# Pacing transfers from small ScalarE copies in the first gated product of an encoder layer

## The chip, the cores and the metric

One Trainium2 chip, one of its cores. The metric is the device time of one execution of the whole layer in microseconds (us), as a median over runs. TensorE multiplies, VectorE and ScalarE do elementwise work, GpSimd and SyncE issue transfers here. In profile rows they are PE, DVE, ACT, POOL and SP.

## The reference

One layer in float32: 512 tokens, width 1024, hidden width 2816.

```python
def rmsnorm(x, g):
    y = xf * lax.rsqrt(jnp.mean(xf * xf, axis=-1, keepdims=True) + EPS)
    return y * g
def swiglu_ffn(x, w_gate, w_up, w_down):
    return (jax.nn.silu(x @ w_gate) * (x @ w_up)) @ w_down
...
x = x + 0.5 * swiglu_ffn(rmsnorm(x, ffn1_norm[l]), ffn1_w_gate[l], ffn1_w_up[l], ffn1_w_down[l])
x = x + hybrid_mixer(...)     # chunked attention beside trailing-mean pooling
x = x + 0.5 * swiglu_ffn(rmsnorm(x, ffn2_norm[l]), ffn2_w_gate[l], ffn2_w_up[l], ffn2_w_down[l])
x = rmsnorm(x, final_norm[l])
```

The change is in the two up products, `x @ w_gate` and `x @ w_up` with what makes their operands; nearly all that moves is in the first.

## The kernel before, in words

**Precision.** Each float32 matrix is split into a high and a low part. ScalarE casts the high part (L684 in the up product), VectorE subtracts it to get the low part (L147). A product is three matmuls: high by high, high by low of the tokens, low of the weights by high.

**The up product** (`ffn_up`). There are 22 tiles of the hidden width, in the order `down.order`. The first two are begun together while tokens and weights still land. The next, up to `plain` (5 in the first up product, 4 in the second), are plain: two weight panels W(n,0) (gate) and W(n,1) (up), 48 matmuls of 512 columns for each. From tile 5 on, seven block products of 256 columns (a Strassen-like scheme: operands A11, S1, S2 and so on of the tokens, and 11, 13, 24, 22 of the weights) take the place of eight: 84 matmuls a tile. For them VectorE forms an odd sum (L969) and an even one (L972, L973) of each tile's weights. Tiles 5 to 12 are "listed"; the rest follow in an order written out by hand.

**What sets the order.** In the plain and listed tiles a planner (`Work`) takes jobs with an engine, a cost, a rank and their dependencies, gives each ScalarE and VectorE job a latest start (`latest`), makes that its rank, and plays the list through once. The order in which jobs start there is the order of instructions on each engine; at run time each engine takes its queue in order. A load is a job of `sp` with a lag until it lands.

**The normalisation.** The tokens' squares (ScalarE, L743 and L746) are added on VectorE (L749), split (L824, L827), averaged over channels by two matmuls (L517), and turned into the factor `rb` by ScalarE (L524 to L526) and VectorE (L530, L534). VectorE's evacuations and the block operands need `rb`.

**The down weights' sums.** The block scheme of the down product needs sums of blocks of the down weights. They are made in DRAM by transfers which GpSimd issues: a copy and then an accumulating one into the same `wsum`. `make_sums(after)` issues one portion (one to three transfers) behind a "mark": a GpSimd copy (L1298) of one element of `after`, so that the portion starts no earlier than `after` is written. In the first product `after` was `rb`, five block operands, the `t` tile of each plain tile from 2 on (its finished activation), and the `t` tile of each listed tile (its first read of the accumulator). The pool of `t` tiles has eight slots; a slot is free for its next use when all reads of it are done, the mark's too.

Of the kernel before, what the change touches and what calls it, by code (L numbers as in the profile page):

```python
# [8 lines left out]
F32 = mybir.dt.float32  # L9
# [7 lines left out]
P = 128  # L17
# [41 lines left out]
FIRST_BYTE = 1.8  # L59
RAW_LAG = 8.0  # L60
MORE = 6
MIX_ENGINES = {
    mybir.EngineType.PE, mybir.EngineType.DVE, mybir.EngineType.Activation, mybir.EngineType.Pool,
}
# [2 lines left out]
def layer(  # L67
# [31 lines left out]
    nc = tc.nc  # L99
# [138 lines left out]
    class Job:  # L238
        def __init__(self, no, engine, cost, rank, emit, after, gets, uses, lag, chunk):
            self.engine, self.cost, self.rank, self.emit = engine, cost, rank, emit  # L240
            self.after = [z for z in after if z is not None]
            self.gets, self.uses, self.lag, self.chunk = list(gets), list(uses), lag, chunk
            self.no, self.then, self.waits, self.ready = no, [], len(self.after), 0.0
            self.spare, self.seat, self.t0 = 0.0, 0.0, None

    class Work:

# [15 lines left out]
        def latest(self, rooms):  # L263


            t, users, first = 0.0, {}, {}
            row = sorted((z for z in self.jobs if z.engine == "pe" and z.rank >= 10.0), key=lambda z: z.rank)
            for z in row:
                z.by = t
                t += z.cost  # L270
            for z in self.jobs:
                for key in z.uses:
                    users.setdefault(key, []).append(z)
                for what, key in z.gets:
                    if key not in first.setdefault(what, {}):
                        first[what][key] = z
            further = {}
            for what, n in rooms.items():
                got = first[what]
                if what == "bank":  # L280
                    keys = sorted(got, key=lambda key: getattr(got[key], "by", got[key].seat))
                else:
                    keys = list(got)
                for key, later in zip(keys, keys[n:]):
                    for z in users.get(key, ()):
                        further.setdefault(z.no, []).append(got[later])

            def start_by(z):
                if not hasattr(z, "by"):
                    z.by = None  # L290
                    ends = [start_by(k) - (0.0 if k.engine == z.engine else self.hop) for k in z.then + further.get(z.no, [])]
                    end = min([*ends, t + z.spare])
                    z.by = end - z.cost - z.lag
                return z.by

            for z in self.jobs:
                start_by(z)
                if z.engine in ("act", "dve"):
                    z.rank = z.by
            return t  # L300

        def plan(self, room, free):
# [327 lines left out]
    def ffn_up(norm, wA, down, loaded, in_order, plain, turns=(), early=()):  # L630
# [109 lines left out]
        def square(k, before):  # L740
            def first():
                norm.acc = tpool.tile([P, S], F32, tag="acc", name=name("acc"), bufs=1)
                nc.scalar.activation(norm.acc, x[k], AF.Square)  # L743

            def emit():
                nc.scalar.activation(buf["sq", k], x[k], AF.Square)  # L746

            def add():
                nc.vector.tensor_tensor(norm.acc, norm.acc, buf["sq", k], op=ALU.add)  # L749

            if before is None:
                return job("act", 0.56, rank["acc"], first, [at_x[k], gain_in])
            z = job("act", 0.56, rank["acc"] + k, emit, [at_x[k]], [("t", ("sq", k))])
            return job("dve", 0.61, rank["acc"] + k, add, [z, before], uses=[("sq", k)])

        def chunk(kp):
# [90 lines left out]

        placed = {}

        def add_sums(f, done):  # L850
            k, second = down.pair(f)
            if second:
                job("dve", 0.78, rank["second"], lambda: down.sums(f), [done, placed[k]])
            placed[k] = done

        def evacuate(n, f, gate, up, after):
            g, sg = ("g", n), ("sg", n)
            z = job(
                "dve", 0.62, rank["evac"],
                lambda: nc.vector.tensor_tensor(  # L860
                    natural(buf[g]), ordered(buf[gate]), natural(norm.rb), op=ALU.mult
                ),
                [at_rb, *after], [("t", g)], [gate],
            )
            z = job(
                "act", 0.57, rank["evac"], lambda: nc.scalar.activation(buf[sg], buf[g], AF.Silu),
                [z], [("t", sg)], [g],
            )
            z = job(
                "dve", 0.61, rank["evac"],  # L870
                lambda: nc.vector.tensor_tensor(buf[sg], buf[sg], norm.rb, op=ALU.mult), [z],
            )
            done = job(
                "dve", 0.61, rank["place"], lambda: down.place(f, ordered(buf[up]), buf[sg]), [z],
                uses=[up, sg],
            )
            add_sums(f, done)
            if n >= 2:
                job("pool", 3.2, n, lambda: down.make_sums(buf[sg]), [done])

        for i in range(2):
            evacuate(i, down.order[i], ("first", 2 * i), ("first", 2 * i + 1), at_first[2 * i : 2 * i + 2])
# [7 lines left out]
            job("pool", 2.8, 0, lambda k=k: put_aside(buf["turned", k], k), [z], uses=[("turned", k)], lag=3.5)  # L890

        freed = [None] * KD
        for n in range(2, plain):
            f, lows = down.order[n], []
            for j in range(2):
                key = ("W", n, j)
                kind = ("praw", "wraw")[j % 2 == 0]
                z = load(wA[2 * f + j], lambda key=key: buf[key][:, :1024], 0.45, 1.3, [(kind, key)])
                lows.append(
                    split_jobs(key, lambda key=key: buf[key][:, :1024], 1024, rank["plain"], [z], [key])  # L900
                )
            units = [(k, j) for k in range(KD) for j in range(2)]
            if n < plain - 1:
                units.sort(key=lambda u: u[1])
            last = [None] * 2
            for k, j in units:

                def unit(n=n, k=k, j=j):
                    w = buf["part", ("W", n, j)]()
                    mm3(buf["plain", n, j], cut(w, k * P, P), norm.h[k], k == 0, k == KD - 1)  # L910

                last[j] = job(
                    "pe", 0.648, filler(), unit, [lows[j][1], last[j]],
                    [("bank", ("plain", n, j))], [("part", ("W", n, j))],
                )
                if n == plain - 1 and j:
                    freed[k] = last[j]
            evacuate(n, f, ("plain", n, 0), ("plain", n, 1), last)
# [5 lines left out]
        used = {k: [turned[k]] if k in turned else [] for k in range(KD)}  # L924
        at_a = norm.blocks(down.pool, aside, work, at_rb, used, freed)

        if not loaded:
            for i, (z, after) in enumerate(
                (
                    (at_rb, lambda: norm.rb),  # L930
                    (at_a[S3][0][0], lambda: work.buf["whole", S3][0][:, 0].bitcast(F32)),
                    (at_a[A11][0][0], lambda: norm.a[A11][0][0].bitcast(F32)),
                    (at_a[S2][0][0], lambda: work.buf["whole", S2][0][:, 0].bitcast(F32)),
                    (at_a[A22][0][0], lambda: norm.a[A22][0][0].bitcast(F32)),
                    (at_a[S1][0][0], lambda: norm.a[S1][0][0].bitcast(F32)),
                )
            ):
                job("pool", 3.2, 1 + 0.1 * i, lambda after=after: down.make_sums(after()), [z])

        raws, w = {}, {}  # L940

# [84 lines left out]
        def operands(n):  # L1026
# [2 lines left out]
            raw = ("raw", n)  # L1029
            at_raw = job(  # L1030
                "sp", 0.9, n_loads[0] + n, lambda: fetch_into(buf[raw], down.order[n]), [],
                [("praw", raw)], lag=2.6 if n < plain + 2 else RAW_LAG,
            )

            def made(i, src, cols, deps, uses):
# [20 lines left out]
        def half_tile(n):  # L1056
# [34 lines left out]

            p = multiply(acc, 11, 0, A11, True, [])
            u_lo = read(u, 0, acc, 1.0, [p])
            job("pool", 3.2, n, lambda: down.make_sums(buf[u][:, :HT]), [u_lo])
            p = multiply(up_hi, 13, S, S3, True, [])
            z_hi = read(z, 1, up_hi, -1.0, [p])
            p = multiply(acc, 24, 0, S2, False, [u_lo])
# [136 lines left out]
    class Down:  # L1234
# [56 lines left out]
        def make_sums(self, after):  # L1291

            at = self.n_sums
            self.n_sums += 1
            part = self.steps[self.bounds[at] : self.bounds[at + 1]]
            with tc.manual_schedule(engines={mybir.EngineType.Pool}):
                mark = small.tile([P, 16], F32, tag="mark", name=name("mark"))
                nc.gpsimd.tensor_copy(mark[:, 0:1], after[:, 0:1])  # L1298
                for _, at, i, g in part:
                    nc.gpsimd.dma_start(  # L1300
                        self.rows(i, g), self.rows(self.terms[i][at], g),
                        **(dict(accum_op=ALU.add) if at else {}),
                    )
# [1258 lines left out]
```

## Time and profile before

| | us |
|---|---|
| median of 3 runs | 806.54 (806.04 to 808.33) |
| the profiled execution | 802.69 |
| its span, from the first to the last instruction | 800.9 |
| TensorE busy | 790.1 |
| VectorE busy | 712.4 |
| ScalarE busy | 498.7 |
| GpSimd busy | 158.5 |

The first up product runs from the start to about 205 us, its listed part to about 136; the second from about 483. Timeline rows give start, duration, engine, line, operation, output and inputs, and in brackets the engine's idle time just before and what ended it. Waits give the sum, the count and the longest. Rows of stretches give length, busy time (and instructions), granted clock, share of the transfer engines and GB/s.

### The profile page before, as it was taken

What the parts mean: (1) busy time and instruction counts of PE and PEld (TensorE: products, weight loads), DVE (VectorE), ACT (ScalarE), POOL (GpSimd) and SP (SyncE); (2) the same over time, 40 slices, a digit from 0 to 9 for tenths busy, and PEclk for the clock granted to TensorE, in tenths of its full rate; (3) what the DMA queues carried; (4) which work ended last, traced back from release to release, by engine and by line L of the source; (5) the groups of instructions that cost most, each with busy time, mean ns of one, the idle gap of its engine ahead of it and who ended that gap; (6) DMA issues with size and microseconds to landing.
All of it is one profiled execution on the core that took longest, in us unless ns stands there. A gap on an engine that the chain in (4) does not pass through costs nothing.

```text
span 800.9 us, 14970 instructions
## 1 busy us (share of the span) xinstructions
PE 790.1 (99%) x5706; PEld 746.2 (93%) x5706; DVE 712.4 (89%) x1117; ACT 498.7 (62%) x858; POOL 158.5 (20%) x246
## 2 busy tenths in 40 slices
PE   9999999999999999999999999999999999999996
PEld 7889899999999999888888888899999999988986
DVE  7899899999988998777699799999999999986997
ACT  7556565555666665557769555455666555766584
POOL 0035321122220000232254245021110011200010
PEclk9999999999999999999999999999999999999998
DMA  8469977698898765585655867145774467869642
GB/s 298 149 170 308 284 214 196 164 240 198 227 280 288 219 201 162 173 264 117 163 191 107 185 178 212 57 151 194 174 186 165 159 173 176 260 238 339 215 140 106
DMA packets 73992, 158.57 MB, mean 198 GB/s; under 512 B 6576, under 2 KB 31680, under 8 KB 73536
## 3 DMA queue, kind: packets, MB, share of 16 engines
q1 hardware_dynamic: 49952, 109.09, 40.3%
q0 software_dynamic: 23680, 48.24, 28.1%
q8 instruction: 45, 0.74, 0.4%
q10 hardware_dynamic: 288, 0.27, 0.1%
q14 instruction: 27, 0.22, 0.1%
HBM read 153.38 MB, written 50.34 MB: 254 GB/s over the span
## 4 chain that ended last, share of the span: by engine, by line
PE 85%; DVE 2%; DMA 1%; issue 1%; ACT 0%; SPq 0%; ACTq 0%; DVEq 0%
PE mm L217 12%; PE mm L219 12%; PE mm L218 12%; PE mm L226 10%; PE a L218 9%; PE a L217 9%; PE a L219 9%; PE a L226 6%; DMA raw<-wsum 1%; PE mm L2005 1%; PE mm L2095 1%; PE a L2069 1%; DVE parts L147 1%; PE mm L2069 0%; PE a L2095 0%
## 5 line engine op out<-in xcount | busy, mean ns | idle before, releaser
L147 DVE TENSOR_TENSOR parts<-raw,parts 128x1024 fp32r<-128x1024 f32 (+2 forms) x129 | 137.3, 1078 | 14.3 <-ACT parts L141 12.2
L1018 ACT ACTIVATE t<-mm 128x256 f32<-128x256 f32 x93 | 35.8, 385 | 86.6 <-PE mm L219 59.7
L141 ACT CAST parts<-raw 128x1024 fp32r<-128x1024 f32 (+1 forms) x60 | 59.3, 993 | 32.7 <-DMA raw<-wsum 10.3
L1298 POOL COPY mark<-t 128x1 f32<-128x1 f32 x40 | 24.9, 622 | 268.1 <-DVE t L1193 149.5
L1300 POOL DMA_DIRECT2D wsum<-in_wB_dram x72 | 73.0, 1146 | 12.6 <-DMA wsum<-wsum 7.5
L684 ACT CAST parts<-raw 128x1024 fp32r<-128x1024 f32 (+2 forms) x69 | 59.8, 883 | 17.8 <-PE a L218 8.0
L147 DVE TENSOR_TENSOR wlo<-raw,whi 128x1024 fp32r<-128x1024 f32 (+1 forms) x41 | 46.8, 1141 | 6.3 <-ACT whi L141 4.3
L147 DVE TENSOR_TENSOR ah<-acts,ah 128x512 fp32r<-128x512 f32 (+1 forms) x72 | 47.1, 663 | 3.0 <-ACT ah L141 2.9
L141 ACT CAST ah<-acts 128x512 fp32r<-128x512 f32 (+1 forms) x72 | 41.0, 583 | 8.6 <-PE mm L218 6.1
L219 PE MATMUL mm<-ha,parts 128*128 128x256 f32 x152 | 41.9, 276 | 0.8 <-DVE parts L147 0.8
L1598 DVE TENSOR_TENSOR parts<-raw,parts 128x1024 fp32r<-128x1024 f32 x24 | 29.6, 1239 | 14.7 <-ACT parts L1593 14.7
L217 PE MATMUL mm<-ha,parts 128*128 128x256 f32 x152 | 41.8, 275 | 0.0
L218 PE MATMUL mm<-ha,parts 128*128 128x256 f32 x152 | 41.8, 275 | 0.0
L1593 ACT CAST parts<-raw 128x1024 fp32r<-128x1024 f32 x24 | 25.2, 1048 | 25.9 <-PE a L218 7.1
L226 PE MATMUL mm<-ha,parts 128*128 128x256 f32 x312 | 38.6, 275 | 0.0
L217 PE MATMUL mm<-ah,parts 128*128 128x256 f32 x136 | 37.4, 275 | 0.0
L218 PE MATMUL mm<-ah,parts 128*128 128x256 f32 x136 | 37.4, 275 | 0.0
L219 PE MATMUL mm<-ah,parts 128*128 128x256 f32 x136 | 37.4, 275 | 0.0
L226 PEld LDWEIGHTS mm<-ha,parts 128*128 128x128 f32 x312 | 36.8, 192 | 0.1
L1018 ACT ACTIVATE t<-a 128x256 f32<-128x256 f32 x47 | 18.1, 384 | 29.5 <-PE a L226 21.2
L963 DVE TENSOR_TENSOR parts<-wsum,parts 128x1024 fp32r<-128x1024 f32 x26 | 31.7, 1219 | 2.6 <-ACT parts L958 2.6
L226 PE MATMUL a<-ha,parts 128*128 128x256 f32 x264 | 32.6, 275 | 0.0
(410 smaller groups left out, 3013.6 us busy)
## 6 DMA issues: line engine op xcount, KB each, us to landing
raw<-in_wA_dram SPq DMA_DIRECT2D x86, 512.0 KB, 5.1
wsum<-in_wB_dram POOLq DMA_DIRECT2D x60, 512.0 KB, 7.7
raw<-wsum SPq DMA_DIRECT2D x36, 512.0 KB, 4.9
raw<-in_wB_dram SPq DMA_DIRECT2D x30, 512.0 KB, 4.9
wsum<-wsum POOLq DMA_DIRECT2D x20, 512.0 KB, 4.8
x<-in_xT_dram SPq DMA_DIRECT2D x16, 256.0 KB, 5.3
raw<-in_wQK_dram SPq DMA_DIRECT2D x8, 512.0 KB, 4.1
wsum<-in_wB_dram POOLq DMA_DIRECT2D x12, 256.0 KB, 7.6
```

What stands on the lines that cost most here:

```text
L141: nc.scalar.copy(hi, src)
L147: nc.vector.tensor_tensor(lo, src, hi.bitcast(F32), op=ALU.subtract)
L217: nc.tensor.matmul(acc, a[0], high, start=start, stop=False, **more)
L218: nc.tensor.matmul(acc, a[0], low, start=False, stop=False, **more)
L219: nc.tensor.matmul(acc, a[1], high, start=False, stop=stop, **more)
L226: nc.tensor.matmul(acc, a[1 if i == 2 else 0], moved, start=start, stop=stop, **more)
L684: "act", c_high, rank_of, lambda: nc.scalar.copy(pair()[0], src()),
L963: nc.vector.tensor_tensor(lo, src, hi.bitcast(F32), op=ALU.subtract)
L1018: nc.scalar.activation(natural(dst), ordered(src), AF.Copy, scale=scale)
L1300: nc.gpsimd.dma_start(self.rows(i, g), self.rows(self.terms[i][at], g), **(dict(accum_op=ALU.add) if at else {}),)
L1593: return lambda: nc.scalar.copy(buf["part", i][0], buf["raw", i])
L1598: nc.vector.tensor_tensor(lo, buf["raw", i], hi.bitcast(F32), op=ALU.subtract)
```

## The change

`pace` adds a 128x1 copy on ScalarE, from what a portion of sums follows, to a tile of its own with four slots; the mark reads that tile. In the first product the portions now follow the high parts of the plain weights from W(2,1) on (five), four block operands (S3, S2, A22, S1), and the listed tiles' first reads (eight): 17 as before. In the second they follow W(2,0), W(3,0) and the eight listed tiles. The small copies are taken from the list as soon as their input is written (`at_once`). The squares, their sums and the mean get a rank 10 us earlier. The first two squares wait for a weight cast. The lag of the first two listed loads in the list goes from 2.6 to 8.0 us. The mark's tile is 8 elements wide and not 16.

```diff
+EARLY_MEAN = 10.0
...
-                    z.rank = z.by
+                    z.rank = -1e3 if z.at_once else z.by - EARLY_MEAN * (z.rank < -5.0 and z.rank >= -19.0)
...
-                return job("act", 0.56, rank["acc"], first, [at_x[k], gain_in])
-            z = job("act", 0.56, rank["acc"] + k, emit, [at_x[k]], [("t", ("sq", k))])
+                return job("act", 0.56, rank["acc"], first, [at_x[k], at_w[0][0][0]])
+            then = at_w[0][3][0] if k == 1 else None
+            z = job("act", 0.56, rank["acc"] + k, emit, [at_x[k], then], [("t", ("sq", k))])
...
+        def pace(at, order, src):
+            n = next(paces)
+            def note():
+                buf["pace", n] = small.tile([P, 1], F32, tag="pace", name=name("pace"), bufs=4)
+                nc.scalar.copy(buf["pace", n], src())
+            z = job("act", 0.22, rank["copy"], note, [at])
+            z.at_once = True
+            job("pool", 3.2, order, lambda: down.make_sums(buf["pace", n]), [z])
...
-            if n >= 2:
-                job("pool", 3.2, n, lambda: down.make_sums(buf[sg]), [done])
...
-        if not loaded:
-            for i, (z, after) in enumerate(
...
-                job("pool", 3.2, 1 + 0.1 * i, lambda after=after: down.make_sums(after()), [z])
+        at_weights = [z for pair in plain_lows[(0 if loaded else 1) :: (2 if loaded else 1)] for z in pair[:1]]
+        if loaded:
+            for i, (z, what) in enumerate(zip(at_weights, plain_keys[::2])):
+                pace(z, i, lambda what=what: buf["part", what](0, 0)[0][:, 0:1].bitcast(F32))
+        else:
+            for i, (z, what) in enumerate(zip(at_weights, plain_keys[1:])):
+                pace(z, i, lambda what=what: buf["part", what](0, 0)[0][:, 0:1].bitcast(F32))
+            for i, what in enumerate((S3, S2, A22, S1)):
+                pace(at_a[what][0][0], 10 + i, lambda what=what: norm.a[what][0][0][:, 0:1].bitcast(F32))
...
-                [("praw", raw)], lag=2.6 if n < plain + 2 else RAW_LAG,
+                [("praw", raw)], lag=RAW_LAG,
...
-            job("pool", 3.2, n, lambda: down.make_sums(buf[u][:, :HT]), [u_lo])
+            pace(u_lo, 20 + n, lambda: buf[u][:, 0:1])
...
-                mark = small.tile([P, 16], F32, tag="mark", name=name("mark"))
+                mark = small.tile([P, 8], F32, tag="mark", name=name("mark"))
```

ScalarE, before, in listed tile 7 (L1018 reads an accumulator into a `t` tile, L1109 and L1116 are the two Silu halves, L684 the casts of the next weights):

```order
L1018 ACTIVATE t_975<-mm_951 128x256 [waits PE_49,Activation_49]
L1109 ACTIVATE t_992<-t_732 128x256 [waits DVE_49,Pool_49]
L1018 ACTIVATE t_997<-mm_967 128x256 [waits PE_49,Activation_49]
L1116 ACTIVATE t_992<-mm_682 128x256
L1018 ACTIVATE t_975<-mm_951 128x256 [waits PE_49]
L1109 ACTIVATE t_1032<-t_860 128x256 [waits DVE_49,Pool_49]
L684 CAST parts<-raw_874 128x512 [waits DMAHW6_49]
```

The same place after:

```order
L1032 ACTIVATE t_998<-a_980 128x256 [waits PE_49]
L858 COPY pace_1004<-t_998 128x1 [waits Activation_49,Pool_49]
L1123 ACTIVATE t_1009<-t_775 128x256 [waits DVE_49]
L1130 ACTIVATE t_1009<-mm_723 128x256
L1032 ACTIVATE t_1026<-mm_995 128x256 [waits PE_49]
L1032 ACTIVATE t_998<-a_980 128x256 [waits PE_49]
L1123 ACTIVATE t_1052<-t_899 128x256 [waits DVE_49]
```

The wait for GpSimd went from the Silus (L1109, now L1123) to the small copy.

VectorE, before, from the last token tile's low part to the low part of the squares' sum (`raw_244`, `raw_276`, `raw_301` are W(2,0), W(2,1), W(3,0)):

```order
L149 SCALAR_TENSOR_TENSOR hlo_315<-x_82,gain_sb,hhi_314 128x512
L147 TENSOR_TENSOR parts<-raw_244,parts 128x1024
L147 TENSOR_TENSOR parts<-raw_276,parts 128x1024
L749 TENSOR_TENSOR acc_182<-acc_182,t_327 128x512
L749 TENSOR_TENSOR acc_182<-acc_182,t_341 128x512
L749 TENSOR_TENSOR acc_182<-acc_182,t_348 128x512
L147 TENSOR_TENSOR parts<-raw_301,parts 128x1024
L827 TENSOR_TENSOR t_372<-acc_182,t_371 128x512
```

The same place after:

```order
L150 SCALAR_TENSOR_TENSOR hlo_311<-x_82,gain_sb,hhi_310 128x512
L750 TENSOR_TENSOR acc_190<-acc_190,t_316 128x512
L750 TENSOR_TENSOR acc_190<-acc_190,t_321 128x512
L750 TENSOR_TENSOR acc_190<-acc_190,t_327 128x512
L750 TENSOR_TENSOR acc_190<-acc_190,t_341 128x512
L148 TENSOR_TENSOR parts<-raw_238,parts 128x1024
L148 TENSOR_TENSOR parts<-raw_271,parts 128x1024
L829 TENSOR_TENSOR t_358<-acc_190,t_357 128x512
L148 TENSOR_TENSOR parts<-raw_303,parts 128x1024
```

The additions went ahead of the low parts of W(2,0) and W(2,1), and the low part of W(3,0) behind the mean's.

VectorE, before, at the end of the listed tiles (L1316, L1317 and L1371 are differences of finished activations; the row `parts<-raw_1515` is the low part of 11 of tile 13):

```order
L972 TENSOR_TENSOR raw_1687<-raw_1664,raw_1515 128x512
L973 TENSOR_TENSOR raw_1687<-raw_1687,raw_1515 128x512
L1105 TENSOR_TENSOR t_1645<-t_1645 128x256
L1316 TENSOR_TENSOR acts_168<-acts_168 128x256
L1317 TENSOR_TENSOR acts_168<-acts_168 128x256
L1086 TENSOR_TENSOR t_1601<-mm_1597,t_1601 128x256
L1086 TENSOR_TENSOR t_1601<-mm_1692,t_1601 128x256
L147 TENSOR_TENSOR parts<-raw_1515,parts 128x512
```

The same place after (`raw_1550` is that tile's):

```order
L986 TENSOR_TENSOR raw_1716<-raw_1703,raw_1550 128x512
L987 TENSOR_TENSOR raw_1716<-raw_1716,raw_1550 128x512
L1330 TENSOR_TENSOR acts_168<-acts_168 128x256
L1331 TENSOR_TENSOR acts_168<-acts_168 128x256
L1385 TENSOR_TENSOR acts_168<-acts_168 128x512
L1119 TENSOR_TENSOR t_1680<-t_1680 128x256
L1100 TENSOR_TENSOR t_1635<-mm_1631,t_1635 128x256
L1100 TENSOR_TENSOR t_1635<-mm_1726,t_1635 128x256
L148 TENSOR_TENSOR parts<-raw_1550,parts 128x512
```

A second L1371 (now L1385) moved from behind that low part to ahead of it; before, it stood seven rows behind.

More of the change, by code (lines that the diff above doesn't have):

```diff
@@ L243, in __init__ @@
             self.no, self.then, self.waits, self.ready = no, [], len(self.after), 0.0
-            self.spare, self.seat, self.t0 = 0.0, 0.0, None
+            self.spare, self.seat, self.t0, self.at_once = 0.0, 0.0, None, False
     class Work:
@@ L848, in ffn_up @@
         placed = {}
+        def pace(at, order, src):
[6 more added lines that the diff above has]
+            job("pool", 3.2, order, lambda: down.make_sums(buf["pace", n]), [z])
+        paces = iter(range(100))
         def add_sums(f, done):
@@ L892, in ffn_up @@
         freed = [None] * KD
+        plain_lows, plain_keys = [], []
         for n in range(2, plain):
-            f, lows = down.order[n], []
+            f, lows = down.order[n], plain_lows[len(plain_lows) :]
             for j in range(2):
@@ L901, in ffn_up @@
                 )
+                plain_lows.append(lows[-1])
+                plain_keys.append(key)
             units = [(k, j) for k in range(KD) for j in range(2)]
@@ L925, in ffn_up @@
         at_a = norm.blocks(down.pool, aside, work, at_rb, used, freed)
-        if not loaded:
-            for i, (z, after) in enumerate(
[L929 to L937, printed above, removed]
-                job("pool", 3.2, 1 + 0.1 * i, lambda after=after: down.make_sums(after()), [z])
+        at_weights = [z for pair in plain_lows[(0 if loaded else 1) :: (2 if loaded else 1)] for z in pair[:1]]
[7 more added lines that the diff above has]
+                pace(at_a[what][0][0], 10 + i, lambda what=what: norm.a[what][0][0][:, 0:1].bitcast(F32))
         raws, w = {}, {}
```

## The prediction

> **What bounds the kernel now.** I read the page's first part, then the waits of TensorE, then busy time by stretches, then the timeline where TensorE stops.
>
> ```profile
> PE 790.1 (99%) x5706; PEld 746.2 (93%) x5706; DVE 712.4 (89%) x1117; ACT 498.7 (62%) x858; POOL 158.5 (20%) x246
> ```
>
> ```profile
> PE mm L226 <- ACT t L1018: 1.9, 1, 1.9
> ...
> PE mm L219 <- DVE parts L147: 0.8, 1, 0.8
> PE mm L226 <- ACT parts L684: 0.3, 1, 0.3
> ```
>
> ```profile
> 80.00:85.00 5.00, 4.86 (x44) 1.00 1.21 230
> 85.00:90.00 5.00, 3.25 (x29) 1.00 1.08 394
> ...
> 135.00:140.00 5.00, 4.15 (x38) 1.00 0.04 13
> ...
> 540.00:550.00 10.00, 10.00 (x92) 1.00 0.69 246
> ```
>
> TensorE is the bound: 790.1 of 800.9 us. In each row of the last fence the fourth number is its busy time in the stretch. It is less than the stretch in three places that matter: two in the first up product (around 85 and 135 us) and 0.3 us at the start. The second up product (540 is inside it) is full, so nothing can be gained there. A change to the first product can win at most these three places.
>
> Around 85 us, engine by engine (start, duration, what, and in brackets the idle time before it and who ended it):
>
> ```profile
> 83.36 1.50 PE L226 MATMUL mm<-ha,parts 128*128 128x256 f32 x12
> 86.75 1.49 PE L226 MATMUL mm<-sa,parts 128*128 128x256 f32 x11 [1.89 <-ACT t L1018]
> ...
> 84.49 0.51 POOL L1300 DMA_DIRECT2D wsum<-wsum  x1 [4.96 <-DMA wsum<-in_wB_dram]
> 84.98 0.20 POOL L1298 COPY mark<-t 128x1 f32<-128x1 f32 x1
> ...
> 80.88 0.38 ACT L1018 ACTIVATE t<-mm 128x256 f32<-128x256 f32 x1 [0.62 <-PE mm L226]
> 85.22 0.42 ACT L1109 ACTIVATE t<-t 128x256 f32<-128x256 f32 x1 [3.96 <-POOL mark L1298]
> 86.32 0.37 ACT L1018 ACTIVATE t<-mm 128x256 f32<-128x256 f32 x1
> ...
> 82.19 1.23 DVE L969 TENSOR_TENSOR raw<-raw 128x1024 f32<-128x1024 f32 x1 [0.25 <-DMA raw<-in_wA_dram]
> 86.17 0.69 DVE L147 TENSOR_TENSOR parts<-raw,parts 128x512 fp32r<-128x512 f32 x1 [1.31 <-ACT parts L684]
> 87.66 1.23 DVE L147 TENSOR_TENSOR wlo<-raw,whi 128x1024 fp32r<-128x1024 f32 x1 [0.80 <-ACT whi L684]
> ```
>
> Read it from the bottom of the chain. GpSimd stands 4.96 us for a sum's transfer; the mark behind it in its queue still has to read a `t` tile (the finished activation of plain tile 4), so that slot is not free; ScalarE's next Silu, L1109, wants the slot and waits 3.96 us; the read of the accumulator behind it in ScalarE's queue, at 86.32, comes late; TensorE waits for it. Twelve products of this shape take 1.34 us (1.50 less the overlap of the last), so TensorE was due at 84.70 and began at 86.75: 2.05 us. VectorE loses 1.31 + 0.80 = 2.11 us to the same block, and 0.25 to a landing.
>
> Around 135 us:
>
> ```profile
> 135.20 0.28 PE L218 MATMUL mm<-ha,parts 128*128 128x256 f32 x1
> 136.32 0.38 PE L219 MATMUL mm<-ha,parts 128*128 128x256 f32 x1 [0.85 <-DVE parts L147]
> ...
> 135.59 0.68 DVE L147 TENSOR_TENSOR parts<-raw,parts 128x512 fp32r<-128x512 f32 x1
> ```
>
> Products start every 0.11 us, so the third was due at 135.31 and came 1.01 us late: VectorE finished its low weights at 136.27, after a queue without a gap since 88.8. VectorE is the second bound of this stage.
>
> **The change part by part.** *Marks read a tile of their own.* No `t` tile is held by GpSimd any more. L1109 then follows its input at about 81.3, the read of the accumulator follows its product (done at 83.4) and is over before 84.70. TensorE regains 2.05 us and VectorE 2.11. The transfers still wait as long; only GpSimd's own queue stands behind them.
>
> *The small copies.* 27 copies on ScalarE (17 in the first product, 10 in the second) take the places of reads that GpSimd did. The nearest row for one is the 128x1 ACTIVATE, the nearest for waiting on one's own engine's last write is a cast:
>
> ```profile
> 30.08 0.20 ACT L441 ACTIVATE table<-t 128x1 f32<-128x1 f32 x1
> ...
> 67.41 1.06 ACT L684 CAST parts<-raw 128x1024 fp32r<-128x1024 f32 x1 [0.35 <-ACT parts L684]
> ```
>
> So 0.20 to 0.55 us each, 3.4 to 9.4 us in the first product. ScalarE is 62% busy, and a copy stands behind the read that feeds TensorE, not ahead of it; the next read is due a product (1.34 us) later. Cost to TensorE: nothing; were that cover gone, up to 0.55 us at each of eight listed tiles. Each copy from the fifth on also waits until GpSimd has read the tile four marks earlier; see the rivals.
>
> *The mean earlier.* Rank minus 10 puts the sums of squares, and the low part of their sum, ahead of the low part of W(3,0) on VectorE; the two mean products stand four products (0.86 us) earlier on TensorE.
>
> ```profile
> 25.09 0.59 PE L517 MATMUL a<-t,mean_of 128*128 128x512 f32 x2
> ...
> 23.11 1.22 DVE L147 TENSOR_TENSOR parts<-raw,parts 128x1024 fp32r<-128x1024 f32 x1
> 24.24 0.69 DVE L827 TENSOR_TENSOR t<-acc,t 128x512 fp32r<-128x512 f32 x1
> 27.86 0.69 DVE L530 SCALAR_TENSOR_TENSOR t<-a,t 128x512 f32<-128x512 f32 x1 [2.93 <-ACT t L526]
> ```
>
> The low part ended at 24.93; with 1.13 us (23.11 to 24.24) less ahead of it, it ends at 23.8, before TensorE's new place at 24.23. So the chain through ScalarE and VectorE's L530 comes about 0.8 us sooner, and VectorE's whole queue behind it, which then runs without a gap. Bounds: 0 (a square comes late) to 0.86.
>
> *The start.* ScalarE casts the quarter weights before the squares; on VectorE the second quarter's low part now stands behind both operations on the second token tile. The page allows a gain of 0.3 (its wait on ACT parts) and a loss of one quarter's 0.42; I take a loss of 0.1 on TensorE. It is hidden: at 135 us TensorE waits for VectorE anyway.
>
> *Later landings (lag 8.0 for the first two listed loads).* They move VectorE's rows, no transfer. The odd sum of listed tile 6 (L969, 1.13 us) passes ahead of the low part of 24 of tile 5:
>
> ```profile
> 60.58 1.50 PE L226 MATMUL mm<-xa,parts 128*128 128x256 f32 x12
> ...
> 58.91 2.35 DVE L147 TENSOR_TENSOR parts<-raw,parts 128x1024 fp32r<-128x1024 f32 x2
> ```
>
> The low part ended near 60.1 and is needed at 60.80 (third product). Now 60.1 + 1.13 - 0.8 = 60.4: 0.4 us to spare. And one `acts` difference (L1371) moves ahead of the low part of tile 13:
>
> ```profile
> 141.93 0.68 DVE L1371 TENSOR_TENSOR acts<-acts 128x512 f32<-128x512 f32 x1
> ```
>
> It costs 0.6 in the queue, between nothing (were VectorE ahead there) and 0.68.
>
> *The second product.* Same edits, full before; 0, from 0 to a loss of 0.5 (a small copy in the wrong place).
>
> *The sum.* It is set by VectorE at tile 13. Its low part ended at 136.27; less 2.11, less 0.8, plus 0.6 gives 133.96, less up to 0.25 if the load of 82.19 lands sooner. TensorE, due at 135.31 - 2.05 + 0.1 = 133.36, then starts about 133.9 instead of 136.32: 2.4 us sooner, of which 0.5 us of waiting is left. Ends: 3.0 (all but the start's 0.1 of 2.05 + 1.01) and 1.9 (0.5 of new short waits on VectorE). After 136 us TensorE is full to the tail, so this carries to the end. The profiled execution took 802.69 us, 3.85 below the median of 806.54; I take the difference off the median: 806.5 - 2.4 = **804.1 us**, and 803.5 to 804.6 for this case.
>
> **Rivals.** *VectorE's new order holds the gain back.* If a late square keeps the mean where it was, the low part of 24 ends at 61.2 and TensorE waits 0.4 at 60.80, and tile 13's comes at 134.76: gain 1.5, **805.0**. For it: the 0.4 us to spare. Against: nothing but one square stands between.
>
> *The sums crowd the first listed loads.* Sums now start near 21 us instead of 29, beside loads that had the queues nearly alone. Loads and sums, transfers started in 20 to 60 us and then in 60 to 90 us, KB each and median to landing:
>
> ```profile
> raw<-in_wA_dram SPq DMA_DIRECT2D x6, 512.0 KB, 4.6
> wsum<-in_wB_dram POOLq DMA_DIRECT2D x6, 512.0 KB, 7.9
> ```
>
> ```profile
> wsum<-in_wB_dram POOLq DMA_DIRECT2D x9, 512.0 KB, 10.3
> raw<-in_wA_dram SPq DMA_DIRECT2D x6, 512.0 KB, 7.3
> ...
> wsum<-in_wB_dram POOLq DMA_DIRECT2D x1, 256.0 KB, 13.4
> ```
>
> ```profile
> 30.44 0.33 SPq L950 DMA_DIRECT2D raw<-in_wA_dram  x1
> 70.92 0.33 SPq L950 DMA_DIRECT2D raw<-in_wA_dram  x1
> ...
> 42.94 1.22 DVE L969 TENSOR_TENSOR raw<-raw 128x1024 f32<-128x1024 f32 x1
> ```
>
> A load in the crowd took 7.3, the worst from 70.92 to its user at 82.19, 11.3 us. The first listed load, issued near 30.9, would at 11.3 land at 42.2, just when VectorE wants it (42.94 - 0.8). At 13.4, the slowest sum, it lands at 44.3: VectorE 2.1 late, and it hardly catches up; **806.2**. Against: few sums are in flight by 31 us. The Trainium skill, "DMA: Bandwidth & Descriptors", section "Issuing engines are not separate DMA queues", says that transfers from all engines run on the same 16 and interleave, which speaks against putting sums here. By an equal share, an estimate from that page and the 4.6 us above, a load beside two sums takes 13.8 us and the time is 806.6. The 7.3 us of the crowded stretch agrees with the direction, not with so large a factor.
>
> *Slower: the block comes back on ScalarE.* With four tiles, a copy waits if GpSimd is over four marks behind, and then not one slot but ScalarE's whole queue stands, once a tile. Each costs what it did at 85 us, 2.05; three make 806.5 + 2 x 2.05 = **810.6**, and three is where it decides. GpSimd falls behind if marks take over a listed tile's 9.38 us (84 products of 0.1117).
>
> ```profile
> 63.84 0.41 POOL L1298 COPY mark<-ha 128x1 f32<-128x1 f32 x1
> 85.73 0.32 POOL L1298 COPY mark<-t 128x1 f32<-128x1 f32 x1
> ```
>
> Between these, with GpSimd behind all the time, five more marks ran: 21.9 us for six steps, 3.65 each. So it catches up; only much slower transfers would do it.
>
> *More than forecast.* The runs' median is 3.85 us above the profiled execution. If part of that is the same block lasting longer when a transfer is slower, the change wins it too: about **801.7**. Nothing in the one profile shows it.
>
> **How the numbers follow.** As forecast 0.50, VectorE's order 0.17, crowd 0.08, slower 0.11, more 0.14. About 0.3% (2.4 us) is what a measurement of this kernel tells from no change, and the forecast lies on that line: a little over half of its 0.50 counts as faster. Faster 0.28 + 0.14 = 0.42; same 0.22 + 0.17 + 0.08 = 0.47; slower 0.11. The range reaches to the crowd above, with the runs' own scatter (806.04 to 808.33), and to the last rival below: 801.0 to 807.2, which leaves out the slower case and the tails.
>
> **What would show it.** Right: no ScalarE wait on a mark, TensorE full from 80 to 90 us, L530 near 27, a wait under 0.8 us for VectorE near 133 to 134, first mark near 21. Wrong: ScalarE copies that wait on GpSimd; VectorE waiting for a landing near 42; TensorE idle near 60; any gap past 480 us.

## The result

The changed kernel takes 801.08 us (median of 6 runs, 800.63 to 801.20), the kernel before, run beside it, 806.04 (median of 5 runs, 803.99 to 808.33): 5.0 us less, a ratio of 0.9937 (95% interval 0.9919 to 0.9954). Three runs in the slow state are left out of the ratios: a sixth one of the kernel before (888.49 us) here, and two of old_sums (814.87 and 815.51) below. The forecast was 804.1 us, with 801.0 to 807.2 as the range. The profiled execution took 800.86 us, against 802.69 before: only 1.83 us less. This difference between 5.0 and 1.83 is what the experiments had to settle.

The profile after. First part, waits of TensorE, and busy time of TensorE by stretches (length, busy time, granted clock, transfers):

```profile
PE 790.6 (99%) x5706; PEld 746.3 (93%) x5706; DVE 712.7 (89%) x1117; ACT 503.9 (63%) x885; POOL 163.1 (20%) x246
...
PE mm L220 <- DVE parts L148: 0.4, 1, 0.4
PE a L219 <- DVE wlo L148: 0.2, 1, 0.2
...
80.00:85.00 5.00, 5.00 (x48) 1.00 0.83 228
85.00:90.00 5.00, 5.00 (x47) 1.00 1.20 192
120.00:130.00 10.00, 9.86 (x89) 1.00 1.13 237
130.00:135.00 5.00, 4.59 (x42) 1.00 0.58 201
...
540.00:550.00 10.00, 10.00 (x92) 1.00 0.58 216
```

The hole at 85 us is closed, and no wait on a mark is left. At 120 to 135 us the busy time is 0.55 us short of the stretches. By the starts of the products, as the prediction counted, the loss there is nearer 1 us: the last record before a stop runs for 0.28 us, though products otherwise start every 0.11 us, so part of each stop counts as busy. Timelines of the places that the forecast spoke of (start, duration, what):

```profile
23.79 0.69 DVE L829 TENSOR_TENSOR t<-acc,t 128x512 fp32r<-128x512 f32 x1
27.19 0.69 DVE L531 SCALAR_TENSOR_TENSOR t<-a,t 128x512 f32<-128x512 f32 x1 [1.57 <-PE mm L227]
42.34 1.22 DVE L983 TENSOR_TENSOR raw<-raw 128x1024 f32<-128x1024 f32 x1
...
120.26 0.68 DVE L1385 TENSOR_TENSOR acts<-acts 128x512 f32<-128x512 f32 x1
131.99 0.68 DVE L1385 TENSOR_TENSOR acts<-acts 128x512 f32<-128x512 f32 x1
133.59 0.68 DVE L148 TENSOR_TENSOR parts<-raw,parts 128x512 fp32r<-128x512 f32 x1
...
24.06 0.96 PE L518 MATMUL a<-t,mean_of 128*128 128x512 f32 x2
122.41 1.91 PE L227 MATMUL mm<-ha,parts 128*128 128x256 f32 x12
133.64 0.28 PE L219 MATMUL mm<-ha,parts 128*128 128x256 f32 x1
134.33 0.38 PE L220 MATMUL mm<-ha,parts 128*128 128x256 f32 x1 [0.41 <-DVE parts L148]
...
21.28 0.37 POOL L1312 COPY mark<-pace 128x1 f32<-128x1 f32 x1 [19.47 <-ACT pace L858]
79.54 0.18 POOL L1312 COPY mark<-pace 128x1 f32<-128x1 f32 x1 [5.12 <-ACT t L1123]
```

L531 came at 27.19 (27.86 before), tile 13's third product at 134.33 (136.32 before), 1.99 us sooner. Three stops are left in these rows: 0.36 us inside the two products of the mean (0.96 us for the pair, 0.59 before), 0.4 us inside the twelve of tile 12 at 122.41 (1.91 us, where such a group takes 1.50), and 0.58 us at tile 13 (due at 133.64 + 0.11 = 133.75). From 79.5 us on GpSimd waits for its marks, so it is no longer behind. The loads of tile weights started in 20 to 60 us now have company (KB each, median to landing):

```profile
wsum<-in_wB_dram POOLq DMA_DIRECT2D x9, 512.0 KB, 8.4
raw<-in_wA_dram SPq DMA_DIRECT2D x6, 512.0 KB, 7.2
```

They landed in 7.2 us instead of 4.6, and VectorE's first user of one, at 42.34, had no idle time before it.

### The profile page after: what moved, and what is told of

Its sections match the earlier page's. It is cut to its first block, busy times and chain, and to the rows that moved or that the text cites. A ratio compares the mean times of both kernels' runs of the same rounds, so it can differ in the third digit from the quotient of the medians.

```text
span 799.1 us, 14937 instructions
## 1 busy us (share of the span) xinstructions
PE 790.6 (99%) x5706; PEld 746.3 (93%) x5706; DVE 712.7 (89%) x1117; ACT 503.9 (63%) x885; POOL 163.1 (20%) x246
## 4 chain that ended last, share of the span: by engine, by line
PE 90%; DVE 6%; issue 1%; DMA 1%; ACT 1%; SPq 0%; DVEq 0%; ACTq 0%
PE mm L218 13%; PE mm L220 13%; PE mm L219 13%; PE mm L227 11%; PE a L218 10%; PE a L219 10%; PE a L220 10%; PE a L227 6%; DVE parts L148 1%; DVE wlo L148 1%; PE mm L2109 1%; PE mm L2019 1%; DMA x<-in_xT_dram 1%; PE a L2083 1%; DVE raw L983 1%
## 5 line engine op out<-in xcount | busy, mean ns | idle before, releaser
L1312 POOL COPY mark<-pace 128x1 f32<-128x1 f32 x27 | 24.7, 915 | 150.3 <-ACT pace L858 145.2
L227 PE MATMUL mm<-ha,parts 128*128 128x256 f32 x336 | 42.2, 275 | 0.1
L220 PE MATMUL mm<-ha,parts 128*128 128x256 f32 x152 | 41.9, 276 | 0.4 <-DVE parts L148 0.4
L218 PE MATMUL mm<-ha,parts 128*128 128x256 f32 x152 | 41.8, 275 | 0.0
L219 PE MATMUL mm<-ha,parts 128*128 128x256 f32 x152 | 41.8, 275 | 0.0
L227 PEld LDWEIGHTS mm<-ha,parts 128*128 128x128 f32 x336 | 39.9, 192 | 0.4 <-DVE parts L148 0.3
L1312 POOL COPY mark<-t 128x1 f32<-128x1 f32 x19 | 6.9, 362 | 157.9 <-DVE t L1207 148.4
```

The lines of the kernel that those rows point to most:

```text
L218: nc.tensor.matmul(acc, a[0], high, start=start, stop=False, **more)
L219: nc.tensor.matmul(acc, a[0], low, start=False, stop=False, **more)
L220: nc.tensor.matmul(acc, a[1], high, start=False, stop=stop, **more)
L227: nc.tensor.matmul(acc, a[1 if i == 2 else 0], moved, start=start, stop=stop, **more)
```

## The experiments

Each was timed against the kernel before on the same chip. Those from one call share the runs of the kernel before, which scattered from 802.27 to 810.49 us in the three calls.

| kernel | us, median (range) | ratio to before (95%) |
|---|---|---|
| before_again | 806.19 (801.95 to 807.12) | 0.9992 (0.9971 to 1.0014) |
| marks_only | 801.42 (799.99 to 803.74) | 0.9945 (0.9927 to 0.9964) |
| direct_marks | 801.06 (800.51 to 801.81) | 0.9941 (0.9918 to 0.9964) |
| mean_later | 800.97 (800.27 to 801.41) | 0.9934 (0.9909 to 0.9960) |
| early_only | 801.36 (800.74 to 802.25) | 0.9950 (0.9932 to 0.9968) |
| old_sums | 813.67 (802.68 to 815.51) | 1.0069 (1.0037 to 1.0102) |
| old_start | 801.01 (800.16 to 801.98) | 0.9938 (0.9913 to 0.9963) |
| sums_later | 800.67 (800.33 to 801.12) | 0.9938 (0.9914 to 0.9962) |
| after_again | 800.96 (800.28 to 801.63) | 0.9941 (0.9922 to 0.9961) |
| last_later | 800.06 (799.71 to 800.89) | 0.9930 (0.9909 to 0.9950) |
| one_tile | 802.41 (801.52 to 803.12) | 0.9953 (0.9935 to 0.9972) |
| marks_one_tile | 810.06 (808.80 to 810.93) | 1.0053 (1.0033 to 1.0073) |

### The kernel before, once more

No edit.

> The kernel before, unchanged, to see another of its executions. The profiled one of 802.69 us lost 2.05 us of TensorE to one block (a Silu of ScalarE that waits for a mark of GpSimd), while the median is 806.3. Theory A (such blocks make the difference too): ratio 1.00, runs scattered over some 4 us, and if the profiled execution is above 804 us, its TensorE waits for ScalarE's L1018 (behind L1109 waiting for a mark) come to more than 1.9 us, up to 1.9 + 3.6. Theory B (the difference has another place): the waits behind marks stay near 1.9 us, and a slower execution loses its time elsewhere, in the down products or at the tail.

Its profiled execution took 807.12 us (span 805.3). Its waits, then ScalarE, TensorE and GpSimd around the block, then TensorE by stretches of 2 us:

```profile
ACT t L1109 <- POOL mark L1298: 5.6, 1, 5.6
ACT t L866 <- POOL mark L1298: 3.0, 1, 3.0
ACT t L1018 <- POOL mark L1298: 1.3, 1, 1.3
...
87.78 0.42 ACT L1109 ACTIVATE t<-t 128x256 f32<-128x256 f32 x1 [5.56 <-POOL mark L1298]
...
73.66 1.50 PE L226 MATMUL a<-ha,parts 128*128 128x256 f32 x12
75.99 1.60 PE L226 MATMUL a<-sa,parts 128*128 128x256 f32 x12 [0.83 <-ACT t L1018]
84.31 1.50 PE L226 MATMUL mm<-ha,parts 128*128 128x256 f32 x12
89.31 2.62 PE L226 MATMUL mm<-sa,parts 128*128 128x256 f32 x12 [3.49 <-ACT t L1018]
91.73 2.15 PE L226 MATMUL mm<-ha,parts 128*128 128x256 f32 x12
93.72 0.39 PE L226 MATMUL a<-xa,whi 128*128 128x256 f32 x2
...
87.05 0.51 POOL L1300 DMA_DIRECT2D wsum<-wsum  x1 [6.46 <-DMA wsum<-in_wB_dram]
87.55 0.20 POOL L1298 COPY mark<-t 128x1 f32<-128x1 f32 x1
...
88.00:90.00 2.00, 0.69 (x4) 0.92 1.17 306
90.00:92.00 2.00, 2.00 (x12) 0.50 1.28 420
92.00:94.00 2.00, 2.00 (x15) 0.73 0.84 299
94.00:96.00 2.00, 2.00 (x20) 1.00 1.20 218
```

It is the block of the prediction in a longer edition. GpSimd waited 6.46 us for a sum's transfer (4.96 in the execution first shown), L1109 5.56 us for the mark, and TensorE, due at 84.31 + 1.34 = 85.65, began at 89.31: 3.66 us. Then comes a price that I had not counted. The granted clock fell to 0.50, and the next two groups of twelve took 2.42 and 1.99 us instead of 1.34 each, 1.73 us more. With 0.99 us at 75.99 (due at 75.00) the blocks cost 6.38 us in this execution, against 2.05 in the first. The Trainium skill, "TensorE: Matmul & The Clock Gate", "What's actually happening", says that an idle window of about 3.4 us halves the clock until TensorE has been busy as long. The trace agrees: the stop of 3.66 us brought 0.50, which was over by 94 us, and the stop of 2.05 us left 1.00. Without the blocks the two executions come out alike: 807.12 - 6.38 = 800.74 us and 802.69 - 2.05 = 800.64. None of its twelve runs was longer than this one, so the median loses less than 6.38. The mean granted clock of the unprofiled runs points the same way: in the 30 runs of the kernel before in this call it was 0.998 to 0.999 in those under 804 us and 0.994 to 0.996 in those from 809 us on. Theory A holds; theory B has nothing for it here.

### Small copies alone

The order of before on all engines, plus 27 copies at the old places (the mark's tile is 8 elements wide here too):

```diff
-                job("pool", 3.2, n, lambda: down.make_sums(buf[sg]), [done])
+                pace(done, n, lambda: buf[sg][:, 0:1])
...
-                job("pool", 3.2, 1 + 0.1 * i, lambda after=after: down.make_sums(after()), [z])
+                pace(z, 1 + 0.1 * i, lambda after=after: after()[:, 0:1])
...
-            job("pool", 3.2, n, lambda: down.make_sums(buf[u][:, :HT]), [u_lo])
+            pace(u_lo, n, lambda: buf[u][:, 0:1])
```

> The kernel before with its order kept on every engine, to which only the 27 small copies are added, at the places where the marks stood, and the marks read them. No earlier sums, no earlier mean, no changed landings. Theory A (the slots that marks held): 801 to 802 us, at most 0.8 above the changed kernel, runs within 1 us of each other, no ScalarE wait on a mark; TensorE waits 0.7 to 0.9 us at tile 13, since VectorE's order is as it was. Theory B (the order and the earlier sums bring it): 805 to 806.5 us, scattered as before.

801.42 us, as theory A said, but the runs scattered over 3.75 us, not within 1. No wait on a mark was left. What TensorE still waits for in the listed tiles is VectorE, and VectorE waits for landings (waits, then one of the two places):

```profile
PE mm L219 <- DVE parts L147: 0.9, 1, 0.9
PE a L226 <- DVE parts L147: 0.7, 1, 0.7
PE a L218 <- DVE wlo L147: 0.6, 1, 0.6
...
82.97 1.23 DVE L983 TENSOR_TENSOR raw<-raw 128x1024 f32<-128x1024 f32 x1 [0.92 <-DMA raw<-in_wA_dram]
```

So the copies alone take the block away. The sums still start late, and loads started in 60 to 90 us took a median of 7.2 us to land (7.3 before). That this crowd makes the scatter is likely, but not shown.

### Earlier sums alone, and marks that read the tiles

Two kernels for the other half. direct_marks is the changed kernel with its order and copies, but the marks read the tiles themselves:

```diff
-            job("pool", 3.2, order, lambda: down.make_sums(buf["pace", n]), [z])
+            job("pool", 3.2, order, lambda: down.make_sums(src()), [z])
```

> The changed kernel with its order kept on every engine, the small copies too, but GpSimd's marks read the cast weights, block operands and t tiles themselves, not the copies. Theory A: holders are blocked again; 803 to 806 us, runs scattered by 2 us or more, and ScalarE or VectorE waits for marks in the profile that stand ahead of TensorE waits. Theory B: the changed kernel's 801.1 us, within 0.5, and runs within 1 us.

801.06 us: my theory A missed here. Marks that hold cast weights, block operands and the first reads of listed tiles cost nothing in this kernel. So a held slot as such is not enough, and theory C followed: GpSimd must also be behind. early_only puts it to the test in the order of before, without a copy:

```diff
-                    (at_rb, lambda: norm.rb),
-                    (at_a[S3][0][0], lambda: work.buf["whole", S3][0][:, 0].bitcast(F32)),
...
+            for i, (z, what) in enumerate(zip([pair[0] for pair in plain_lows[1:]], plain_keys[1:])):
+                job("pool", 3.2, i, lambda what=what: down.make_sums(buf["part", what](0, 0)[0][:, 0:1].bitcast(F32)), [z])
...
-            if n >= 2:
+            if n >= 2 and loaded:
                 job("pool", 3.2, n, lambda: down.make_sums(buf[sg]), [done])
```

> The kernel before with its order kept on TensorE, VectorE, ScalarE and SyncE; only the marks of the first product move to the changed kernel's earlier places (cast weights, block operands), read there directly, without small copies. In the listed tiles they read the t tiles as before. Theory C (two conditions make the block: GpSimd is behind when the listed tiles begin, and a mark holds a slot; taking away either ends it): 801 to 802 us, runs within 1.5 us, no wait of ScalarE on a mark longer than 0.5 us. Rival D (the earlier sums need the changed order or the copies beside them): 803 to 806 us, scattered, with waits on marks.

801.36 us, no wait of ScalarE on a mark. GpSimd in early_only, mark for the first read of tile 7:

```profile
78.73 0.21 POOL L1294 COPY mark<-t 128x1 f32<-128x1 f32 x1 [8.54 <-ACT t L1014]
```

It waited for its tile; in the execution of before shown above, GpSimd was so far behind that the mark of plain tile 4, older than this one, ended at 87.75. Theory C fits: with nothing but copies, or nothing but earlier sums, nearly the whole gain is there, and both together bring little more. One thing is left open. The slot of the block was that of a plain tile's finished activation, and neither direct_marks nor early_only has a mark that reads such a tile. So early_only takes away both the lateness and this hold; earlier sums with the marks of the plain tiles left in place were not tried.

### All but the sums

The changed kernel with marks at the old places, reading the tiles:

```diff
-            pace(u_lo, 20 + n, lambda: buf[u][:, 0:1])
+            job("pool", 3.2, n, lambda: down.make_sums(buf[u][:, :HT]), [u_lo])
```

and likewise at the other places.

> The changed kernel with the marks as before: at the old places, reading the tiles themselves, no small copies. The earlier mean, the start, the landings and the planner stay as changed, so this is all of the change but its handling of the sums. Theory C: 804.5 to 806.5 us, scattered over 2 us or more, with waits on marks as in the kernel before. Rival E (the other edits bring a part of their own): 801.5 to 803.5 us.

813.67 us, slower than before, worse than either theory. ScalarE and TensorE in it, then TensorE by stretches:

```profile
81.58 0.42 ACT L1128 ACTIVATE t<-t 128x256 f32<-128x256 f32 x1 [12.44 <-POOL mark L1317]
82.59 2.93 PE L227 MATMUL a<-ha,parts 128*128 128x256 f32 x12 [11.33 <-ACT t L1037]
...
78.00:80.00 2.00, 0.00 (x0) 0.50 1.22 208
88.00:90.00 2.00, 2.00 (x20) 1.00 1.06 141
```

In the order that came out, the Silu that wants a held slot stands earlier, behind tile 6's first read, and waits 12.44 us. The planner does not know that GpSimd is behind. The loss is not the same in every execution: one of the twelve runs took 802.68 us, two 807 to 808, the others 812 and more. So the other edits bring nothing without the sums, and a block of the same kind took another size. The order on TensorE, VectorE and ScalarE differs from that of the changed kernel as well as from that of before, so the loss against before is that of this order with late sums, not of one edit.

### The earlier mean and the start

mean_later and old_start undo one edit each:

```diff
-EARLY_MEAN = 10.0
+EARLY_MEAN = 0.0
```

> The changed kernel with the earlier rank of the squares and of the mean set to nothing. As I worked it out, VectorE's chain of the mean (L531) comes 0.7 us later, its queue has no gap behind it, and tile 13's low part is later by as much: 801.8 us (801.5 to 802.2), TensorE waiting 1.1 us instead of 0.4 there. Rival (VectorE's queue has slack in between): 801.1 us, no change. Second rival (the low part of 24 of tile 5 comes late too): above 802.2.

```diff
-                return job("act", 0.56, rank["acc"], first, [at_x[k], at_w[0][0][0]])
-            then = at_w[0][3][0] if k == 1 else None
+                return job("act", 0.56, rank["acc"], first, [at_x[k], gain_in])
+            then = None
```

> The changed kernel with the first two squares as before, not behind a weight cast. In the changed kernel TensorE stood 0.17 us further at 21 us than before. If the start carries to the end: 801.25 us, 0.1 to 0.3 above the changed kernel. If VectorE sets the time at tile 13, which I hold likelier: 801.1 us, no difference above 0.15, and TensorE's wait at tile 13 shorter by what it lost at the start.

Neither moves the time. In mean_later VectorE's L531 came 0.91 us later, and yet tile 13's third product was not later than in the changed kernel (134.33):

```profile
28.10 0.69 DVE L531 SCALAR_TENSOR_TENSOR t<-a,t 128x512 f32<-128x512 f32 x1 [3.11 <-ACT t L527]
134.01 0.38 PE L220 MATMUL mm<-ha,parts 128*128 128x256 f32 x1 [0.68 <-DVE parts L148]
```

TensorE also came to tile 13 sooner, its first product there at 132.94 (133.53 in the changed kernel), and waited longer. Each of the two kernels has a VectorE order of its own, so this shows only that the 0.8 us of the mean does not carry through to tile 13.

### One slot for the small copies

```diff
-                buf["pace", n] = small.tile([P, 1], F32, tag="pace", name=name("pace"), bufs=4)
+                buf["pace", n] = small.tile([P, 1], F32, tag="pace", name=name("pace"), bufs=1)
```

In the changed kernel:

> The changed kernel with one slot for the small copies' tiles instead of four: a copy waits until GpSimd's mark has read the one before, and ScalarE's queue stands behind it. By the changed kernel's profile (ninth copy at 55.25, eighth mark over at 63.57) that copy waits 8.3 us, and the reads of the first accumulators (L1032 at 59.63) stand behind it. Theory (a mark held by one slot blocks ScalarE as a t tile did): 804 to 809 us, scattered. Rival (GpSimd is never far behind, that mark's long duration is a matter of the profile): 801.1 us.

In the kernel before with small copies:

> The kernel before with the small copies at the old places (marks_only), and one slot for their tiles instead of four. By that kernel's profile the tenth copy (71.98) would wait for the ninth mark (over at 74.87), 2.9 us, and the thirteenth 0.3 us. Theory: 802.5 to 805.5 us, scattered more than with four slots (800.0 to 803.7). Rival: as with four slots, 801.4 us.

802.41 and 810.06 us: a small loss where GpSimd keeps up, less than I expected, and a large one where it is behind, more than I expected. The waits of ScalarE on marks in one_tile, then in marks_one_tile, and there TensorE behind the longest (timeline and stretches):

```profile
ACT pace L858 <- POOL mark L1312: 1.8, 1, 1.8
```

```profile
ACT pace L856 <- POOL mark L1312: 12.4, 5, 5.0
...
88.45 2.55 PE L226 MATMUL mm<-ha,parts 128*128 128x256 f32 x12 [3.55 <-ACT t L1032]
...
90.00:92.00 2.00, 2.00 (x11) 0.50 1.07 437
```

With one slot the block is back, on the copies. With four slots no profile here shows a copy that waits for GpSimd.

### Room behind tile 13

sums_later puts three pairs of differences of finished activations behind the low part of 11 of tile 13, last_later only the last pair:

```diff
+        if not loaded:
+            for z in seconds[-1:]:
+                wait_for(z, at_part[begun, 11][1])
```

(`seconds` lists the jobs of L1330 and L1331; sums_later has `seconds[-3:]`.)

> The changed kernel with three pairs of operand differences of finished activations (L1330, L1331, L1385; wanted only in the down product) put behind the low part of 11 of tile 13 on VectorE, not ahead of the low parts of tiles 12 and 13. Theory (VectorE's queue sets the last two waits, 0.4 us at tile 12 and 0.7 at tile 13): both waits go, 800.0 us (799.8 to 800.4). Rival (VectorE has no room behind tile 13 either and the waits come back after 136 us): 801 us or more.

> The changed kernel with only the last pair of differences of finished activations (L1330 and L1331, and with them the last L1385; 1.4 us of VectorE) put behind the low part of 11 of tile 13. Three pairs put there took both waits of the changed kernel away and gave a new one of 0.54 us at 140 to 160 us. Theory (VectorE's queue has about 3 us of room behind tile 13): the wait of 0.4 us at tile 13 goes and none comes: 800.7 us (800.5 to 800.9). Rival (no room at all): 801.1 us, the wait found again behind 136 us.

sums_later took 800.67 us: the waits at 120 to 135 us went, and one of 0.54 us came at tile 14, so neither theory was quite right. last_later took 800.06, beside 800.96 of the changed kernel in the same call (ranges 799.71 to 800.89 and 800.28 to 801.63, which overlap). TensorE by stretches in last_later:

```profile
130.00:135.00 5.00, 5.00 (x47) 1.00 0.74 253
140.00:160.00 20.00, 20.00 (x181) 1.00 0.70 176
```

The wait at tile 13 is gone (0.4 us in after_again) and none came behind it. The medians differ by 0.9 us, more than these 0.4; what the other 0.5 is, was not tested. In these two profiles a wait of TensorE for VectorE past 700 us differs too (0.8 in after_again, 0.3 in last_later), far behind the edit. last_later has the lowest median of the study.

> The changed kernel, unchanged, beside the three that follow. 801.1 us (800.6 to 801.4), runs within 1 us of each other. If the changed kernel also had blocks that come in some executions only, some run would be above 802.5.

The six runs of the changed kernel stayed within 1.35 us, none above 801.63.

## Why the prediction was right and wrong

- **Right: the place and the mechanism.** L1109 behind a mark behind a transfer was the loss. Seen before and gone after; marks_only took it away with the order of before kept, and with one slot for the copies it came back on them. early_only took it away too, with the open point said there.
- **Wrong: the base of the sum.** The step that failed is "I take the difference off the median". For the profiled execution the sum gave 2.4 us (1.9 to 3.0) and 1.83 were measured, just under the lower end. But the block of that execution was a short one. In before_again's execution the same block, with a shorter one ahead of it, cost 6.38 us, of which 1.73 came from the halved clock, a term my sum did not have. The 2.05 us of the first term was thus right for one execution and too small for the median, which lies between the two that were traced. The rival "More than forecast" (801.7, given 0.14) described this, and deserved more: a median 3.85 us above the profiled execution, beside a wait on a transfer, was the hint. That 801.08 lies inside the range, by 0.08 us, is owed to this rival, which set the lower end, and to luck; the sum did not lead there.
- **The sum inside the profiled execution.** Its 2.05 us came, but terms beside it were off. TensorE was 0.19 us late when it reached the block (83.55, 83.36 before), 1.86 sooner behind it (84.89, 86.75 before), then lost 0.4 at tile 12, which no term had, and won 0.43 at tile 13 (0.58 of waiting for 1.01). Together that is 1.9 of the 1.99 measured there; the forecast was 2.4.
- **The mean.** L531 came 0.67 us earlier, near the 0.8 forecast, but the term is worth nothing in the end (mean_later). One reading behind it was wrong: the low part ended at 24.48, not at 23.8, because four additions of squares stand ahead of it where three stood before. TensorE, at its new place at 24.06, waited 0.36 us for it, a cost that the term did not have.
- **VectorE at tile 13.** Forecast: low part at 133.96, TensorE at 133.9 with 0.5 us of waiting. Measured: 134.27, 134.33 and 0.58 (0.41 in the row). The L1371 that I had counted came ahead of that low part (now L1385, at 131.99). The other one moved too, which I had not counted: from behind tile 12's low part (before, last row of this fence) to ahead of it (120.26), where TensorE loses 0.4 us now. In sums_later, which puts these differences back behind, that loss is gone.

```profile
123.65 0.68 DVE L147 TENSOR_TENSOR parts<-raw,parts 128x512 fp32r<-128x512 f32 x1
...
128.65 0.68 DVE L1371 TENSOR_TENSOR acts<-acts 128x512 f32<-128x512 f32 x1
```

- **The landings.** I put the moves of VectorE's rows in the first product down to the later landings. With the old lags put back, the changed kernel has the same order of instructions in the first product, so the moves come from its other edits. No run was spent on it.
- **The start.** I took a loss of 0.1. At the same product TensorE stood at 21.03 us, against 21.21 before, but at 20.77 in old_start: so this edit cost it some 0.26 us there, and others brought more than that. In the time, old_start shows no difference.
- **Rival "VectorE's new order".** The odd sum (L983) did go ahead of tile 5's low part of 24, and no wait of TensorE near 60 us came.
- **Rival "the crowd".** Its direction came (7.2 us for 4.6), not its lateness: VectorE did not wait at 42.34. The equal share, an estimate from the Trainium skill, "DMA: Bandwidth & Descriptors", section "Issuing engines are not separate DMA queues", would have given 13.8 us for a load beside two sums; the measurement decides.
- **The slower rival.** Its condition was absent: with four slots no copy waited on GpSimd. That its 810.6 us lies near the 810.06 of marks_one_tile is chance. There one slot on another kernel made TensorE wait 1.02, 1.34 and 3.55 us for ScalarE and brought a stretch at clock 0.50, not three stops of 2.05.
- **The second product.** TensorE stayed full there (540 to 550 us above), as forecast.

## What to carry to other kernels

A wait on a transfer that stands in one engine's queue blocks everything whose buffers that engine still has to read; here giving the reader a small copy cured it, and so did starting the transfers earlier, behind other tiles; one of the two was enough. Where a trace shows a stall whose length hangs on a transfer, one execution does not price it: compare its time with the median, and with a second trace, before the difference is taken off. A reordering that gains nothing by itself can come with a longer stall of this kind (old_sums), so the stall goes first.

## What the runs showed of the hardware

- By the idle time recorded ahead of the restart, a stop of TensorE of 1.89 us left the granted clock at 1.00; stops of 3.49, 3.55 and 11.33 us were followed by stretches at 0.50. After the one of 3.49 us this added 1.73 us.
- One-element copies on GpSimd took from 0.18 us to several us by the profile. One of the changed kernel, and in one_tile another with the ScalarE copy that waited for it:

```profile
55.82 7.75 POOL L1312 COPY mark<-pace 128x1 f32<-128x1 f32 x1
```

```profile
55.32 6.26 POOL L1312 COPY mark<-pace 128x1 f32<-128x1 f32 x1
...
61.61 0.19 ACT L858 COPY pace<-t 128x1 f32<-128x1 f32 x1 [1.79 <-POOL mark L1312]
```

What such a copy itself waits for was not tried.
